# Chunked scans of a two-head block: 64x64 quadrant products against padded 128x128 products, four chains in step

## The chip, the cores and the metric

The kernel runs on one core of one Trainium2 chip. The metric is the device time of one execution in microseconds (us); a shorter time is better. The time before is the median of three runs.

## The reference, cut to what matters

One layer of a hybrid network on 384 tokens (128 context, 256 latent) of width 2048. One large projection makes all inputs; branch A is a bidirectional scan over tokens with a 64x64 state for each of 32 heads, branch B a short convolution, and both are projected out again:

```python
def step(S, inp):                      # for each direction d and head h
    r_t, w_t, k_t, v_t, a_t, b_t = inp
    sa = einsum('dbhij,dbhj->dbhi', S, a_t)
    S = S * w_t[..., None, :] + sa[..., :, None] * b_t[..., None, :] + v_t[..., :, None] * k_t[..., None, :]
    y = einsum('dbhij,dbhj->dbhi', S, r_t)
    return S, y
```

Context scans start at zero, latent scans at given states; the final context states are outputs. The reads of both directions are summed, normed by head, gated and projected.

## The kernel before, in words

**The dense stream.** Every product with a big weight is a step of one stream: a 128x128 tile of the weight against 384 tokens, as three matmuls (lines 81 to 83: high part by high, by low, low by high). A pair of column tiles has 32 steps, in four quarters of 8 steps. The weights of a quarter are loaded by SyncE, cast to the high part by ScalarE (line 88, `whi`) and subtracted to the low part by VectorE (line 89, `wlo`), with three buffers of each: a cast waits until TensorE is through with the quarter three before.

**The scans.** Heads go in 16 blocks of two. In a block each direction's 384 tokens are six chunks of 64: two of the context and four of the latent tokens. So a block has four chains: context and latent (`ch` 0 and 1), forward and backward (`d` 0 and 1). Work inside the chunks comes first: `prep_a` (rates, decays, keys; the last product is `pn`, from which VectorE makes `kn` with three reciprocals), `prep_b` (masked 64x64 matrices `A` by the products `pA`; inverses of their 32x32 corners on VectorE, by way of DRAM), `prep_c` (transposes `pv`, `pb`; products `pav`; states transposed in, `psi`). Then `scan`: the products `pH` and `pX` complete the 64x64 inverses, with copies `x11` between them; `pbn` gives the bonus `bon`. For each chunk of a chain: `po` (state by keys and reads, 128x128), an add on VectorE, `pq` (the solve), copies to `sav` on ScalarE, `pu` (the state update), and two multiply-adds for each chain on VectorE into the state `st`. Next, `py2` adds the reads inside the chunks, `pso` transposes the final context states out, and `norm` and `finish` end the block.

**Quadrants.** `pA` has 64 rows of contraction; `pq`, `pu`, `pav` and `py2` have one product for each head, whose outputs lie in 64 partitions each; `pH` and `pX` are 32x32 products. All of these are float32, and each float32 product stands as two instructions (passes) in the trace; a transpose is one.

**Order.** TensorE's order is written out by hand: `drive` runs the generators of the scans, and each `yield n` puts n dense steps (3n matmuls) into the stream before the next small burst. `PB0, PB1, H0, H1, CH0, CH1` are these numbers. The four chains are advanced two at a time: two chains' bursts, `CH0` steps, the other two chains' bursts. Between `prep_c` and `scan` lie at least `WINDOW` = 80 steps, under which the inverses run. The other engines' order is made by a scheduler when the program is built, and each engine works its list in order.

The matmuls with the dense weights in the shown code are `mm3`; `bank` is one of five PSUM banks.

Of the kernel before, what the change touches and what calls it, by code (L numbers as in the profile page):

```python
# [56 lines left out]
def hybrid_step(ctx, tc, cst, x_prompt, x_sample, state_f, state_b, c, c_ctx, ada_w, ada_b, norm_g,  # L57
# [507 lines left out]
    st = {}
    for d in range(2):
        for ch in range(2):
            s0 = sp.tile([P, P], F32, tag=f"st{d}{ch}", name=f"st{d}{ch}")
            G.memset(s0[:], 0.0)
            st[d, ch] = s0  # L570
# [83 lines left out]
    def prep_b(b, o):  # L654
        """the decayed operands and the masked matrices inside the chunks"""
        r, kk = r_[b], o["kk"]
        o["pr"], o["bk"], o["A"] = [], [], []
# [16 lines left out]
        uo = dp.tile([2, 2, 2, 12, 32, 32], F32, tag="uo", name=f"uo_{b}", bufs=2)  # L674
        for d in range(2):
            pr, bk = o["pr"][d], o["bk"][d]
            A = sp.tile([P, NCH, 2, P], F32, tag=f"A{d}", name=f"A_{b}_{d}")
            m0 = C_MB if d else C_MF
            mk = cs[:, m0:m0 + P].unsqueeze(1).broadcast_to([P, 3, P])
            for n3 in (0, 3):  # L680
                pas = [bank(f"pA_{b}_{d}_{n3}_{h}") for h in range(2)]
                for n in range(3):
                    for h in range(2):
                        TE.matmul(pas[h][:, n, :], bk[hss[h], n3 + n, :], pr[hss[h], n3 + n, :],  # L684
                                  start=True, stop=True)
# [24 lines left out]
        o["x11"] = []  # L710
        for d in range(2):
            A = o["A"][d]
            for e in range(2):
# [4 lines left out]
            nc.sync.dma_start(x11[0:32], uo[1, d, 0].rearrange("i s t -> s i t"))
            o["x11"].append(x11)

    def prep_c(b, o):
        """keys and values by token, the values' part of the removals, the bonus"""
        r, v = r_[b], v_[b]
        o["bkt"], o["sav"] = [], []
        for d in range(2):
            for h in range(2):
                nc.sync.dma_start(s_in[d][hss[h], hss[h]], ctx_st[d][0, 0, 2 * b + h])
        for d in range(2):
            sav = sp.tile([P, NCH, P], F32, tag=f"sav{d}", name=f"sav_{b}_{d}")
# [8 lines left out]
            for e in range(2):  # L738
                S.copy(sav[C:P, e:NCH:2, :], pv[C * e:C * e + C, 0:3, :])
# [1 line left out]
            o["sav"].append(sav)
        for d in range(2):
            bt = sp.tile([P, NCH, P], F32, tag=f"bt{d}", name=f"bt_{b}_{d}")
            # the last latent chunk changes no state that is read
            for n0, n1 in (((0, 3), (3, 5)), ((0, 3), (4, 6)))[d]:
# [3 lines left out]
                S.copy(bt[:, n0:n1, :], pb[:, 0:n1 - n0, :])  # L749
                yield 1  # L750
            o["bkt"].append(bt)
        for d in range(2):
            sav = o["sav"][d]
            for n3 in (0, 3):
                pv = bank(f"pav_{b}_{d}_{n3}")
                for n in range(3):
                    for h in range(2):
                        TE.matmul(pv[hss[h], n, 0:C], o["A"][d][C:P, n3 + n, h, 0:C], sav[C:P, n3 + n, hss[h]],
                                  start=True, stop=True)
                for h in range(2):  # L760
                    S.copy(sav[0:C, n3:n3 + 3, hss[h]], pv[hss[h], 0:3, 0:C])
                yield 1
# [4 lines left out]
        yield 1  # L767
        for d in range(2):
            pt = bank(f"psi_{b}_{d}")
            TE.transpose(pt[:, 0, :], s_in[d][:], ident)  # L770
            V.tensor_copy(st[d, 1][:], pt[:, 0, :])
            yield 1

    def scan(b, o):
        # upper right blocks of the 64x64 inverses, U11*A12*U22; the first product transposed
        for d in range(2):
            A, x11 = o["A"][d], o["x11"][d]
            py = bank(f"pH_{b}_{d}")
            for n in range(NCH):
                for h in range(2):  # L780
                    g = 32 * (2 * (n % 2) + h)
                    TE.matmul(py[g:g + 32, n // 2, 0:32], A[0:32, n, h, 32:64], x11[0:32, 2 * n + h, :],
                              start=True, stop=True)
# [10 lines left out]
        for d in range(2):  # L794
            A, x11 = o["A"][d], o["x11"][d]
            pz = bank(f"pX_{b}_{d}")
            for n in range(NCH):
                for h in range(2):
                    g = 32 * (2 * (n % 2) + h)
                    TE.matmul(pz[g:g + 32, n // 2, 0:32], x11[32:64, 2 * n + h, :], A[32:64, n, h, 32:64],  # L800
                              start=True, stop=True)
            for j in range(4):
                (V.tensor_copy, S.copy)[d](A[0:32, j // 2::2, j % 2, 32:64], pz[32 * j:32 * j + 32, 0:3, 0:32])
            yield H1
# [5 lines left out]
        def chain(d, ch):  # L810
            A, sav, pr, bt, ep = o["A"][d], o["sav"][d], o["pr"][d], o["bkt"][d], o["ep"][d]
            s_ = st[d, ch]
            n0 = ((0, 2), (4, 0))[d][ch]
            cnt = (2, 4)[ch]
            for i in range(cnt):
                n = n0 + i
                zero = ch == 0 and i == 0
                m = n if d == 0 else 5 - n
# [322 lines left out]
```

## Time and profile before

| | us |
|---|---|
| median of three runs (2334.58 to 2335.70) | 2335.09 |
| span of the profiled execution | 2333.0 |
| TensorE busy in the span | 2295.7 (98%) |
| VectorE busy | 1568.7 (67%) |
| ScalarE busy | 1120.9 (48%) |
| 16 blocks, from 190 to 1900 us; one block | 109.4 |

The profile is of one execution; its span leaves out what a run's time has around it (here 2.1 us against the median). PE is TensorE, DVE VectorE, ACT ScalarE, POOL GpSimd, SP SyncE. A row of the timeline has start, duration, engine, line, operation, output<-inputs, shapes and, for instructions in a row that are alike, their count and common duration. A matmul's duration is a latency: the next one starts before it ends, so what a matmul costs is read from one start to the next.

### The profile page before, as it was taken

To read this page: it belongs to the slowest core of one execution; us is meant where nothing else is said; L and a number is where in the kernel's file an instruction comes from. 1 tells how busy PE (TensorE), PEld (TensorE's weight loads), DVE (VectorE), ACT (ScalarE), POOL (GpSimd) and SP (SyncE) were. 2 spreads that over 40 slices of the span, in tenths; PEclk is the share of its full clock that TensorE was granted. 3 is DMA by queue.
4 is the path that set the end of the run, shared out by engine and by line. 5 is a ranking of instruction groups with operands and counts; after the bars stand their busy time and mean duration, and the time that the engine had idled before them with its cause. 6 is when DMAs were issued, how large, how long until landed. Compare 5 with 4: busy or idle time off the path is not lost.

```text
span 2333.0 us, 42495 instructions
## 1 busy us (share of the span) xinstructions
PE 2295.7 (98%) x16788; PEld 2043.7 (88%) x16788; DVE 1568.7 (67%) x3350; ACT 1120.9 (48%) x2342; POOL 81.6 (3%) x83
## 2 busy tenths in 40 slices
PE   5999999999999999999999999999999999999998
PEld 2579999989898989899998989898989989868988
DVE  2258777787777878787877777776868665333444
ACT  3246445454555555464645464555555543223333
POOL 2000000000000000000000000000000000000000
PEclk9999999999999999999999999999999999999999
DMA  9963433434353434343433444343444457774633
GB/s 335 344 177 106 128 103 107 134 101 126 103 138 94 124 106 127 99 121 104 130 105 107 141 116 137 109 140 100 131 118 130 144 175 243 239 257 154 226 133 119
DMA packets 431718, 340.08 MB, mean 146 GB/s; under 512 B 84816, under 2 KB 413088, under 8 KB 430624
## 3 DMA queue, kind: packets, MB, share of 16 engines
q1 hardware_dynamic: 430032, 335.62, 48.2%
q8 instruction: 132, 2.16, 0.4%
q10 hardware_dynamic: 432, 1.57, 0.2%
q14 instruction: 66, 0.54, 0.1%
q0 software_dynamic: 1056, 0.19, 0.1%
HBM read 307.37 MB, written 29.36 MB: 144 GB/s over the span
## 4 chain that ended last, share of the span: by engine, by line
PE 95%; DVE 1%; DMA 1%; SPq 1%; issue 1%; ACT 0%; POOLq 0%; POOL 0%; ACTq 0%
PE d_rk L81 4%; PE d_rk L83 4%; PE d_rk L82 4%; PE d_gv L81 3%; PE d_gv L82 3%; PE d_gv L83 3%; PE d_ma L81 3%; PE d_bc L81 3%; PE d_mb L81 2%; PE d_bg L81 2%; PE d_bx L81 2%; PE d_gb L81 2%; PE pA L684 2%; PE d_oa L81 2%; PE pada L276 2%; PE d_oa L83 2%
## 5 line engine op out<-in xcount | busy, mean ns | idle before, releaser
L701 DVE TENSOR_TENSOR ut<-U 48x30 f32<-48x30 f32 (+14 forms) x480 | 154.3, 322 | 60.6 <-DMA U<-ui 49.5
L81 PE MATMUL d_gv<-h_hi,whi_gv 128*128 128x384 f32 x496 | 165.9, 335 | 0.0
L83 PE MATMUL d_gv<-h_hi,wlo_gv 128*128 128x384 f32 x496 | 165.7, 334 | 0.0
L82 PE MATMUL d_gv<-h_lo,whi_gv 128*128 128x384 f32 x496 | 165.7, 334 | 0.0
L81 PE MATMUL d_rk<-h_hi,whi_rk 128*128 128x384 f32 x480 | 160.6, 335 | 0.6 <-ACT lst L542 0.6
L82 PE MATMUL d_rk<-h_lo,whi_rk 128*128 128x384 f32 x480 | 160.3, 334 | 0.0
L83 PE MATMUL d_rk<-h_hi,wlo_rk 128*128 128x384 f32 x480 | 160.3, 334 | 0.0
L703 DVE TENSOR_TENSOR U<-U,ut 48x30 f32<-48x30 f32 (+14 forms) x480 | 153.8, 320 | 8.9
L88 ACT CAST whi_gv<-raw_gv 128x1024 fp32r<-128x1024 f32 (+1 forms) x64 | 65.7, 1027 | 138.0 <-PE d_rk L82 96.6
L88 ACT CAST whi_rk<-raw_rk 128x1024 fp32r<-128x1024 f32 x60 | 62.9, 1050 | 112.1 <-PE d_rk L82 35.2
L838 ACT ACTIVATE ls<-st,ep 64x64 f32<-64x64 f32 x256 | 88.5, 346 | 52.3 <-DVE st L855 30.5
L89 DVE TENSOR_TENSOR wlo_rk<-raw_rk,whi_rk 128x1024 fp32r<-128x1024 f32 x60 | 73.2, 1220 | 46.3 <-ACT whi_rk L88 46.1
L89 DVE TENSOR_TENSOR wlo_oa<-raw_oa,whi_oa 128x1024 fp32r<-128x1024 f32 x32 | 39.2, 1224 | 91.0 <-ACT whi_oa L88 91.0
L81 PE MATMUL d_bc<-h_hi,whi_bc 128*128 128x384 f32 x256 | 96.9, 379 | 0.0
L81 PE MATMUL d_ma<-h_hi,whi_ma 128*128 128x384 f32 x256 | 96.8, 378 | 0.0
L81 PE MATMUL d_mb<-h_hi,whi_mb 128*128 128x384 f32 x256 | 96.6, 377 | 0.0
L81 PE MATMUL d_gb<-h_hi,whi_gb 128*128 128x384 f32 x256 | 96.1, 375 | 0.0
L81 PE MATMUL d_bx<-h_hi,whi_bx 128*128 128x384 f32 x256 | 95.2, 372 | 0.0
L844 ACT COPY sav<-pq 64x64 f32<-64x64 f32 x384 | 79.4, 207 | 32.9 <-PE pq L842 25.1
L81 PE MATMUL d_bg<-h_hi,whi_bg 128*128 128x384 f32 x256 | 95.0, 371 | 0.0
L81 PEld LDWEIGHTS d_gv<-h_hi,whi_gv 128*128 128x128 f32 x496 | 93.1, 188 | 0.2
L82 PEld LDWEIGHTS d_gv<-h_lo,whi_gv 128*128 128x128 f32 x496 | 93.1, 188 | 0.0
(317 smaller groups left out, 6726.4 us busy)
## 6 DMA issues: line engine op xcount, KB each, us to landing
raw_adah<-in_ada_w_dram SPq DMA_DIRECT2D x64, 512.0 KB, 8.0
raw_gv<-in_w_in_dram SPq DMA_DIRECT2D x62, 512.0 KB, 4.4
raw_rk<-in_w_in_dram SPq DMA_DIRECT2D x60, 512.0 KB, 5.3
raw_bc<-in_w_in_dram SPq DMA_DIRECT2D x16, 1024.0 KB, 5.4
raw_bx<-in_w_in_dram SPq DMA_DIRECT2D x16, 1024.0 KB, 5.5
raw_bg<-in_w_in_dram SPq DMA_DIRECT2D x16, 1024.0 KB, 5.5
raw_gb<-in_w_in_dram SPq DMA_DIRECT2D x16, 1024.0 KB, 5.4
raw_ma<-in_w_in_dram SPq DMA_DIRECT2D x16, 1024.0 KB, 5.4
```

Source lines behind the costliest of these rows:

```text
L81: TE.matmul(out, wh, xh, start=start, stop=False)
L82: TE.matmul(out, wh, xl, start=False, stop=False)
L83: TE.matmul(out, wl, xh, start=False, stop=stop)
L88: S.copy(hi[0:rows], src)
L89: V.tensor_tensor(lo[0:rows], src, hi[0:rows].bitcast(F32), ALU.subtract)
L276: TE.matmul(ps[g:g + 32, 0:512], cw[:, k, :], raw[:, k % 4, :], start=k < 4, stop=k >= KC - 4)
L684: TE.matmul(pas[h][:, n, :], bk[hss[h], n3 + n, :], pr[hss[h], n3 + n, :], start=True, stop=True)
L701: V.tensor_tensor(tv, U[:, 0:s, s:s + 1].broadcast_to([48, s, w]), U[:, s:s + 1, s + 1:].broadcast_to([48, s, w]), ALU.mult)
L703: V.tensor_tensor(U[:, 0:s, s + 1:], U[:, 0:s, s + 1:], tv, ALU.add)
L838: S.mul(ls[hss[h], :], s_[hss[h], hss[h]], lam[hss[h]])
L844: S.copy(sav[0:C, n, hss[h]], pq[hss[h], 0, 0:C])
```

## The change

- The matrices of both heads and both directions stand in one tile `A[P, 12, 2, P]`, heads side by side. The lower half of its solve part is set to zero by GpSimd after `pav` (`G.memset`).
- `pq` and `pu` become one 128x128 product for each chunk (both heads; the off-diagonal 64x64 results aren't read): two passes in place of four.
- The four chains go in step: at each `i` all live chains' `po`, then `CH0` steps, all `pq`, `CH0` steps, all `pu`, `CH1` steps. For i = 0 the context chains have no `po`; for i = 2 and 3 only the latent chains live.
- `pA` goes in two bursts a block instead of four, `pav` in one instead of four, `pH` and `pX` in one each instead of two, `py2` in one instead of three, `psi` in one instead of two. `pso` moves from the end to the place ahead of `po` of i = 2.
- VectorE's adds and ScalarE's copies to `sav` take two chains at once. Half of the `x11` copies go from ScalarE to VectorE, where the ones after `pX` are again half and half.
- The DMAs that carry the 32x32 corners go by head: 8 out and 8 back a block instead of 4 and 4, and 2 for `x11`.
- `PB1, H0, H1, CH0, CH1` go from 3, 2, 1, 2, 2 to 6, 3, 3, 3, 3. Comments are dropped.

```diff
-    PB0, PB1, H0, H1, CH0, CH1 = 14, 3, 2, 1, 2, 2
+    PB0, PB1, H0, H1, CH0, CH1 = 14, 6, 3, 3, 3, 3
...
+        pz = corner("pH", lambda f, h: A[0:32, f, 0, C * h + 32:C * h + C], lambda f, h: x11[0:32, 2 * f + h, :])
+        for j in range(4):
+            (S.copy, V.tensor_copy)[j % 2](x11[32:64, j::4, :], pz[j])
+        yield H0
...
+        pz = corner("pX", lambda f, h: x11[32:64, 2 * f + h, :], lambda f, h: A[32:64, f, 0, C * h + 32:C * h + C])
...
+        for i in range(4):
...
+                for d, f in enumerate(ff):
+                    TE.matmul(po[:, 2 * a + d, :], o["pr"][d][:, f % NCH, :], st[ch][:, d, :], start=True, stop=True)
+            for a, (ch, fs, ff) in enumerate(pairs):
+                if not (ch == 0 and i == 0):
+                    V.tensor_tensor(sav[0:C, fs, :], po[0:C, 2 * a:2 * a + 2, :], sav[0:C, fs, :], ALU.add)
...
+            yield CH0
+            for a, (ch, fs, ff) in enumerate(pairs):
+                for d, f in enumerate(ff):
+                    TE.matmul(pq[:, 2 * a + d, :], A[:, f, 0, :], sav[:, f, :], start=True, stop=True)
+            for a, (ch, fs, ff) in enumerate(pairs):
+                for h in range(2):
+                    S.copy(sav[0:C, fs, hss[h]], pq[hss[h], 2 * a:2 * a + 2, hss[h]])
+            yield CH0
+            if i < 3:
...
+                        TE.matmul(pu[:, 2 * a + d, :], bt[:, f, :], sav[:, f, :], start=True, stop=True)
...
+                                V.scalar_tensor_tensor(st[ch][hs, d, hs], pu[hs, 2 * a + d, hs], lam[hs],
+                                                       lss[f][hs, :], ALU.mult, ALU.add)
+                yield CH1
+            if i == 1:
+                pt = bank(f"pso_{b}")
+                for d in range(2):
+                    TE.transpose(pt[:, d, :], st[0][:, d, :], ident)
```

How VectorE's list changes is seen at two places of block 8, and the names are the same in all middle blocks. The first is between `pn` (of the next block's `prep_a`) and the copies after `pX`. Before:

```order
L631 TENSOR_SCALAR kn_12191<-pn_12188 128x384
L646 TENSOR_SCALAR kd_0_12201<-sig_2_12168,par,omka 128x384
L633 RECIPROCAL kn_12191<-kn_12191 128x128 x3
L792 TENSOR_TENSOR bon_12262<-pbn_12259,v_10837 128x384
L803 COPY A_0_11523<-pX_0_12264 32x3x32 x4
```

And now, where `x_8` is the tile `x11`:

```order
L630 TENSOR_SCALAR kn_11512<-pn_11509 128x384
L645 TENSOR_SCALAR kd_0_11522<-sig_2_11489,par,omka 128x384
L632 RECIPROCAL kn_11512<-kn_11512 128x128
L791 COPY x_8_10994<-pH_11534 32x6x32
L632 RECIPROCAL kn_11512<-kn_11512 128x128
L798 TENSOR_TENSOR bon_11575<-pbn_11572,v_10242 128x384
L791 COPY x_8_10994<-pH_11534 32x6x32
```

The second `x11` copy, without which `pX` can't go past its third product, stands behind two reciprocals and behind `bon`, which needs `pbn`.

The second place is from the add after the latent chains' first `po` to the first state updates. Before:

```order
L827 TENSOR_TENSOR rhs_0_2_12317<-po_0_2_12315,sav_0_11685 64x128
L827 TENSOR_TENSOR rhs_1_0_12325<-po_1_0_12323,sav_1_11706 64x128
L647 TENSOR_TENSOR kd_0_12201<-k_11958,kd_0_12201 128x384
L648 TENSOR_TENSOR sig_2_12168<-kn_12191,sig_2_12168 128x384
L641 SCALAR_TENSOR_TENSOR L_1_12205<-cs,sig_1_12144 128x384
L89 TENSOR_TENSOR wlo_bc_0_0_12284<-raw_bc_0_12281,whi_bc_0_0_12283 128x1024
L646 TENSOR_SCALAR kd_1_12209<-sig_3_12180,par,omka 128x384
L662 TENSOR_TENSOR bk_0_12690<-sig_2_12168,sig_0_12132 128x6x64
L853 TENSOR_SCALAR st_1113<-pu_0_0_12369,ep_1125 64x64 x2
L853 TENSOR_SCALAR st_1117<-pu_1_4_12374,ep_1127 64x64 x2
```

And now:

```order
L827 TENSOR_TENSOR sav_11009<-po_0_11626,sav_11009 64x2x128
L647 TENSOR_TENSOR sig_2_11489<-kn_11512,sig_2_11489 128x384
L89 TENSOR_TENSOR wlo_bc_0_0_11612<-raw_bc_0_11609,whi_bc_0_0_11611 128x1024
L645 TENSOR_SCALAR kd_1_11530<-sig_3_11501,par,omka 128x384
L661 TENSOR_TENSOR bk_0_11924<-sig_2_11489,sig_0_11453 128x6x64
L646 TENSOR_TENSOR kd_1_11530<-k_11279,kd_1_11530 128x384
L647 TENSOR_TENSOR sig_3_11501<-kn_11512,sig_3_11501 128x384
L662 TENSOR_TENSOR bk_0_11924<-kd_0_11522,sig_0_11453 128x6x64
L661 TENSOR_TENSOR bk_1_11930<-sig_3_11501,sig_1_11465 128x6x64
L662 TENSOR_TENSOR bk_1_11930<-kd_1_11530,sig_1_11465 128x6x64
L871 SCALAR_TENSOR_TENSOR st_1115<-pu_0_11665,ep_1121,ls_2_11631 64x64 x2
L871 SCALAR_TENSOR_TENSOR st_1115<-pu_0_11665,ep_1123,ls_6_11634 64x64 x2
```

Nine operations that have nothing to do with the scan stand between the add and the state updates, where six stood. Of the eight state updates of a step only the first waits for TensorE, and it waits for the whole burst `pu`.

More of the change, by code (lines that the diff above doesn't have):

```diff
@@ L562, in hybrid_step @@
     ps1 = ctx_sc.enter_context(tc.tile_pool(name="ps1", bufs=1, space=bass.MemoryType.PSUM))
[L565 to L570, printed above, removed]
+    st = []
+    for ch in range(2):
+        s0 = sp.tile([P, 2, P], F32, tag=f"st{ch}", name=f"st{ch}")
+        G.memset(s0[:], 0.0)
+        st.append(s0)
     s_in = []
@@ L738, in prep_c @@
             for e in range(2):
[L739 removed]
+                S.copy(sav[C:P, NCH * d + e:NCH * d + NCH:2, :], pv[C * e:C * e + C, 0:3, :])
             yield 1
[L741 removed]
         for d in range(2):
[L743 to L745 removed]
+            for n0, n1 in (((0, 4), (4, 5)), ((0, 3), (4, 6)))[d]:
                 pb = bank(f"pb_{b}_{d}_{n0}")
@@ L748, in prep_c @@
                     TE.transpose(pb[:, n - n0, :], o["bk"][d][:, n, :], ident)
-                S.copy(bt[:, n0:n1, :], pb[:, 0:n1 - n0, :])
+                S.copy(bt[:, NCH * d + n0:NCH * d + n1, :], pb[:, 0:n1 - n0, :])
                 yield 1
-            o["bkt"].append(bt)
-        for d in range(2):
[L753 to L762, printed above, removed]
+        pvs = [bank(f"pav_{b}_{d}") for d in range(2)]
+        for f in range(2 * NCH):
+            for h in range(2):
+                TE.matmul(flat(pvs[f // NCH][hss[h]])[:, C * (f % NCH):C * (f % NCH) + C], A[C:P, f, 0, hss[h]],
+                          sav[C:P, f, hss[h]], start=True, stop=True)
+        for d in range(2):
+            for h in range(2):
+                S.copy(sav[0:C, NCH * d:NCH * d + NCH, hss[h]],
+                       flat(pvs[d][hss[h]])[:, 0:NCH * C].rearrange("p (n i) -> p n i", i=C))
+        G.memset(A[C:P, :, 0, :], 0.0)
+        yield 2
         ks = o["kd"]
@@ L793, in scan @@
         o["bon"] = bon
[L794 to L804, printed above, removed]
+        pz = corner("pX", lambda f, h: x11[32:64, 2 * f + h, :], lambda f, h: A[32:64, f, 0, C * h + 32:C * h + C])
+        for j in range(4):
+            (S.copy, V.tensor_copy)[j % 2](A[0:32, j // 2::2, 0, C * (j % 2) + 32:C * (j % 2) + C], pz[j])
+        yield H1
         ytok = sp.tile([P, 3, P], F32, tag="ytok", name=f"ytok_{b}")
@@ L808, in scan @@
         written = set()
[L810 to L818, printed above, removed]
-                q, e = m // 2, m % 2
-                rhs = sav[0:C, n, :]
-                lam = ep[:, n, C:C + 1]
-                need_state = ch == 0 or i < cnt - 1
-                if not zero:
-                    po = ps1.tile([P, 512], F32, tag="A", name=f"po_{b}_{d}_{n}", bufs=5)
-                    TE.matmul(po[:, 0:P], pr[:, n, :], s_[:], start=True, stop=True)
-                    rhs_t = sp.tile([C, P], F32, tag="rhs", name=f"rhs_{b}_{d}_{n}", bufs=2)
-                    V.tensor_tensor(rhs_t[:], po[0:C, 0:P], rhs, ALU.add)
-                    rhs = rhs_t
-                    dst = ytok[C * e:C * e + C, q, :]
+        for i in range(4):
+            pairs = []
+            for ch in (1, 0):
+                if i < (2, 4)[ch]:
+                    n0 = [((0, 2), (4, 0))[d][ch] + i for d in range(2)]
+                    f0, step = n0[0], NCH + n0[1] - n0[0]
+                    pairs.append((ch, slice(f0, f0 + step + 1, step), [f0, f0 + step]))
+            po = bank(f"po_{b}_{i}")
+            pq = bank(f"pq_{b}_{i}")
+            for a, (ch, fs, ff) in enumerate(pairs):
+                if ch == 0 and i == 0:
+                    continue
+                for d, f in enumerate(ff):
[3 more added lines that the diff above has]
+                    V.tensor_tensor(sav[0:C, fs, :], po[0:C, 2 * a:2 * a + 2, :], sav[0:C, fs, :], ALU.add)
+            lss = {}
+            for a, (ch, fs, ff) in enumerate(pairs):
+                for d, f in enumerate(ff):
+                    if ch == 0 and i == 0:
+                        continue
+                    if (ch, i) != (1, 3):
+                        ls = sp.tile([P, C], F32, tag="lam", name=f"ls_{b}_{f}", bufs=4)
+                        lam = o["ep"][d][:, f % NCH, C:C + 1]
+                        for h in range(2):
+                            S.mul(ls[hss[h], :], st[ch][hss[h], d, hss[h]], lam[hss[h]])
+                        lss[f] = ls
+            for a, (ch, fs, ff) in enumerate(pairs):
+                for d, f in enumerate(ff):
+                    if ch == 0 and i == 0:
+                        continue
+                    m = f if d == 0 else 5 - f % NCH
+                    dst = ytok[hss[m % 2], m // 2, :]
@@ L859, in scan @@
-        live = [chain(0, 1), chain(1, 1), chain(0, 0), chain(1, 0)]
-        while live:
-            k = 0
-            for ch in list(live):
-                if next(ch, 1):
-                    live.remove(ch)
-                    if len(live) == 2:
-                        yield CH1 - CH0 + 1
-                else:
-                    k += 1
-                if k == 2 or (k and ch is live[-1]):
-                    yield CH0 if len(live) > 2 else CH1
-                    k = 0
+            yield CH0
@@ new lines, in scan @@
+            if i == 1:
+                pt = bank(f"pso_{b}")
+                for d in range(2):
+                    TE.transpose(pt[:, d, :], st[0][:, d, :], ident)
+                for d in range(2):
+                    nst = sp.tile([P, C], F32, tag="ns", name=f"ns_{b}_{d}")
+                    for h in range(2):
+                        S.copy(nst[hss[h], :], pt[hss[h], d, hss[h]])
+                    nc.sync.dma_start(ctx_ns[d][0, 0, 2 * b:2 * b + 2].rearrange("h i j -> (h i) j"), nst[:])
@@ L877, in scan @@
                     for e in range(2):
-                        n = 2 * q + e if d == 0 else 5 - 2 * q - e
-                        TE.matmul(py[hss[e], q, hss[h]], o["A"][d][:, n, h, C:P], o["sav"][d][:, n, hss[h]],
+                        f = 2 * q + e if d == 0 else NCH + 5 - 2 * q - e
+                        TE.matmul(py[hss[e], q, hss[h]], A[:, f, 1, hss[h]], sav[:, f, hss[h]],
                                   start=d == 0, stop=d == 1)
-            yield 1
+        yield 1
         V.tensor_tensor(ytok[:], ytok[:], py[:, 0:3, :], ALU.add)
-        for d in range(2):
-            pt = bank(f"pso_{b}_{d}")
-            TE.transpose(pt[:, 0, :], st[d, 0][:], ident)
-            nst = sp.tile([P, C], F32, tag="ns", name=f"ns_{b}_{d}")
-            for h in range(2):
-                S.copy(nst[hss[h], :], pt[hss[h], 0, hss[h]])
-            nc.sync.dma_start(ctx_ns[d][0, 0, 2 * b:2 * b + 2].rearrange("h i j -> (h i) j"), nst[:])
     def norm(b, o):
```

113 lines of the change are left out of this document (53 added, 60 removed).

## Prediction

> **What bounds the kernel now.** I read the page's busy times first, then the engines' busy time by stretch, then TensorE's waits, then the timeline of one block. Page, stretch (the 16 blocks; the second row is block 7's scan from its first `po` to `py2`), and the longest waits of TensorE inside the blocks:
>
> ```profile
> span 2333.0 us, 42495 instructions
> ## 1 busy us (share of the span) xinstructions
> PE 2295.7 (98%) x16788; PEld 2043.7 (88%) x16788; DVE 1568.7 (67%) x3350; ACT 1120.9 (48%) x2342; POOL 81.6 (3%) x83
> ```
>
> ```profile
> 190.00:1900.00 1710.00, 1708.10 (x13457) 1575.20 (x13457) 1304.23 (x2919) 905.97 (x1989) 58.69 (x31) 1.00 0.43 120
> ```
>
> ```profile
> 1030.35:1056.37 26.02, 26.02 (x209) 22.28 (x208) 22.21 (x55) 17.05 (x53) 0.00 (x0) 1.00 0.29 86
> ```
>
> ```profile
> PE pA L684 <- DVE bk L662: 1.0, 1, 1.0
> PE pq L842 <- DVE rhs L827: 0.3, 1, 0.3
> ```
>
> TensorE is busy for 1708.1 of the blocks' 1710 us at full clock: every passage of a small burst costs its whole time, and nothing else sets the end. But in the scan VectorE (the third busy time of a stretch's row) is busy too, 22.2 of 26.0 us. A product that has to wait for VectorE there costs as much as one that is too long.
>
> **What a burst costs.** A dense matmul first: these are the first and the last of 58 rows 0.173 us apart (57 intervals in 9.88 us).
>
> ```profile
> 999.68 0.33 PE L83 MATMUL d_gv<-h_hi,wlo_gv 128*128 128x384 f32 x1
> ...
> 1009.56 0.33 PE L83 MATMUL d_gv<-h_hi,wlo_gv 128*128 128x384 f32 x1
> ```
>
> A burst costs the time from the dense matmul ahead of it to the second one behind it, less two dense matmuls (0.35). Five bursts follow: `pq` and `po` of two chains, `py`, `pA`, `pH`, each with those two neighbours.
>
> ```profile
> 1033.29 0.34 PE L83 MATMUL d_bc<-h_hi,wlo_bc 128*128 128x384 f32 x1
> 1033.56 0.45 PE L842 MATMUL pq<-rhs,A 64*64 64x64 f32 x8
> ...
> 1034.22 0.34 PE L82 MATMUL d_bc<-h_lo,whi_bc 128*128 128x384 f32 x1
> ```
>
> ```profile
> 1030.17 0.34 PE L83 MATMUL d_bc<-h_hi,wlo_bc 128*128 128x384 f32 x1
> 1030.35 0.61 PE L825 MATMUL po<-st,pr 128*128 128x128 f32 x4
> ...
> 1030.97 0.34 PE L82 MATMUL d_bc<-h_lo,whi_bc 128*128 128x384 f32 x1
> ```
>
> ```profile
> 1056.10 0.34 PE L83 MATMUL d_bx<-h_hi,wlo_bx 128*128 128x384 f32 x1
> 1056.37 0.69 PE L879 MATMUL py<-sav,A 128*64 128x64 f32 x16
> ...
> 1057.26 0.34 PE L82 MATMUL d_bx<-h_lo,whi_bx 128*128 128x384 f32 x1
> ```
>
> ```profile
> 1070.60 0.34 PE L83 MATMUL d_bg<-h_hi,wlo_bg 128*128 128x384 f32 x1
> 1070.87 0.94 PE L684 MATMUL pA<-pr,bk 64*128 64x128 f32 x12
> ...
> 1072.01 0.34 PE L82 MATMUL d_bg<-h_lo,whi_bg 128*128 128x384 f32 x1
> ```
>
> ```profile
> 1026.17 0.34 PE L83 MATMUL d_bc<-h_hi,wlo_bc 128*128 128x384 f32 x1
> 1026.44 0.39 PE L782 MATMUL pH<-x,A 32*32 32x32 f32 x24
> ...
> 1027.04 0.34 PE L82 MATMUL d_bc<-h_lo,whi_bc 128*128 128x384 f32 x1
> ```
>
> So `pq` (8 passes) costs 0.93 - 0.35 = 0.58, `py` (16) 1.16 - 0.35 = 0.81, `pA` (12) 1.06, `pH` (24) 0.52, `po` (4) 0.45. Between `pq` and `py` eight passes add 0.23, 0.029 each; the rest of `pq`, 0.58 - 8 x 0.029 = 0.35, is what entering and leaving a burst of part-array products costs. With that fixed part a pass of `pA` costs 0.06 and one of `pH` 0.007. `po`, full-array, costs 4 x 0.1135 and has no fixed part to speak of.
>
> **The gain on TensorE, a block.** All of it lies on the path.
> - `pq`: 6 bursts of 0.58 = 3.50; now 12 products, 24 passes of 0.1135 = 2.72. Gain 0.78.
> - `pu`: 10 chain steps. By my reading of the code its form and passes are those of `pq`, so 5 x 0.58 = 2.92; now 20 passes, 2.27. Gain 0.65.
> - `pav`, 4 bursts of 12 passes like `pq`'s: 4 x 0.70 = 2.80; now one of 48: 0.35 + 48 x 0.029 = 1.74. Gain 1.06.
> - `py2`: 3 x 0.81 = 2.44; now one of 48, 1.74. Gain 0.70.
> - `pA`: 4 x 1.06 = 4.25; now 2 of 24: 2 x (0.35 + 1.44) = 3.58. Gain 0.7.
> - `pH` and `pX`: 4 x 0.52 = 2.10; now 2 of 48: 2 x (0.35 + 0.34) = 1.38. Gain 0.7.
> - `po`, `pso`, `psi`: the same passes, nothing.
>
> Together 4.6 us a block, 16 x 4.6 = 74 us. Bounds: 68 to 78, if a pass in a burst of 48 costs 10% more or the fixed part is 0.37.
>
> The Trainium skill, page "TensorEngine Tiling (Array Packing)", section "Performance Considerations", advises to tile the array wherever contraction and columns are 64 or less, since tiles work at the same time; by it the padding of `pq` and `pu` is a step the wrong way. What the rows make of it: per chain step four tiled passes add 0.115 and two full ones 0.227, so padding alone loses 0.11; it wins only because each tiled burst pays 0.35 at its ends. If full products paid that too, 7 bursts x 0.35 x 16 = 39 us of the 74 would go.
>
> **What now comes late.** With pairs of chains out of step, one pair's copies and updates lay under the other pair's burst and four dense steps. With all in step there are only three dense steps, 9 x 0.173 = 1.56 us, between a burst and the one that needs its result, and twice as many results. The durations for three places:
>
> ```profile
> 1024.43 0.34 PE L628 MATMUL pn<-sqh,bones_r 128*128 128x384 f32 x1
> 1024.87 0.39 PE L782 MATMUL pH<-x,A 32*32 32x32 f32 x24
> 1024.98 0.56 DVE L631 TENSOR_SCALAR kn<-pn 128x384 f32<-128x384 f32 x1 [0.53 <-PE pn L629]
> 1025.45 0.47 DVE L646 TENSOR_SCALAR kd<-sig,par,omka 128x384 f32<-128x384 f32 x1
> 1025.84 2.57 DVE L633 RECIPROCAL kn<-kn 128x128 f32<-128x128 f32 x3
> ...
> 1028.46 0.56 DVE L792 TENSOR_TENSOR bon<-pbn,v 128x384 f32<-128x384 f32 x1
> ...
> 1028.93 1.07 DVE L803 COPY A<-pX 32x96 f32<-32x96 f32 x4
> ```
>
> ```profile
> 1030.77 0.51 DVE L827 TENSOR_TENSOR rhs<-po,sav 64x128 f32<-64x128 f32 x2 [0.30 <-PE po L825]
> ```
>
> ```profile
> 1045.06 1.18 DVE L855 SCALAR_TENSOR_TENSOR st<-pu,ep,ls 64x64 f32<-64x64 f32 x4 [0.56 <-PE pu L849]
> ```
>
> ```profile
> 1024.17 1.28 ACT L643 ACT_TABLE_LOAD   x1
> ```
>
> ```profile
> L88 ACT CAST whi_rk<-raw_rk 128x1024 fp32r<-128x1024 f32 x60 | 62.9, 1050 | 112.1 <-PE d_rk L82 35.2
> ...
> L89 DVE TENSOR_TENSOR wlo_rk<-raw_rk,whi_rk 128x1024 fp32r<-128x1024 f32 x60 | 73.2, 1220 | 46.3 <-ACT whi_rk L88 46.1
> ```
>
> The last two are groups of the page: a cast lasts 1.05 us, a `wlo` 1.22.
>
> **Place 1, `pX`.** Count from `pn` at 0. VectorE: `kn` at 0.55, the rates at 1.02, a reciprocal at 1.41 (0.86 each), the first `x11` copy at 2.27 (0.26), a reciprocal until 3.39, `bon` 0.47 more, the second copy until 4.1. TensorE: `pH` at 0.44, 0.69 with its fixed part, nine dense 1.56: `pbn` at 2.7, `pX` due at 3.1. Wait 1.0 us (0.8 to 1.3), new, in the 14 middle blocks.
>
> **Place 2, the second `po`.** Count from the first `po` (4 passes, 0.45). With 1.56 after each burst, `pq` (8 passes, 0.91) starts at 2.0, `pu` at 4.5, the next `po` at 6.95, and its fourth product, at 7.6, needs the last state update. VectorE: the add is through by 1.1 (`po` ends at 0.61; two single adds take 0.51); then eight operations 0.47 apart, as `bon` and the row after it, and a `wlo`: 3.8 + 1.2, free at about 6.0. `pu` ended at 5.5, so the updates start at 6.0. Eight of them 0.30 apart end at 8.4, and the product starts at 8.5. Wait 0.9 (0.4 if VectorE were free, 1.1 if it starts 0.2 late), in the 14 middle blocks.
>
> **Place 3, `pso`.** It now stands ahead of the third `po` and needs all eight updates. From the second `pq` at 0: `pu` at 2.47, ended by 3.5; updates until 5.9 at the earliest; the second transpose is due at 2 x 2.47 + 0.11 = 5.05. Wait 0.9 in every block. In five middle blocks a `wlo` stands ahead of the updates whose cast has to wait until TensorE is two dense steps past `pq`: 2.1 + 1.05 + 1.22 = 4.4, updates until 6.8, wait 1.75; in two others a gate product stands there that waits for ScalarE's last copies, about 2.2. In seven blocks ScalarE loads a table (1.28) ahead of the copies that `pu` needs; I count 0.4 there, between nothing and the whole load. 5 x 1.75, 2 x 2.2, 9 x 1.0 and 7 x 0.4 make 25 us, 1.6 a block (0.9 to 2.2).
>
> Sum: 16 x (1.0 + 0.9 + 1.6) = 56, less 2 for the end blocks: 54 us (34 to 74 by the bounds). Elsewhere I find cover: copies to `sav` (four, at 0.26 as the copies after `pX`, an estimate) end at 1.06 + 1.04 after an eight-pass burst begins, 0.3 before `pu`; the inverses come back early, though ten DMAs go where six went:
>
> ```profile
> 1016.64 0.47 SPq L718 DMA_DIRECT2D x<-uo  x1
> ```
>
> That is the last of the six, issued 8.2 us before `pH` (1024.87); four more at about 0.45 take 1.8 of them. If that cover went, `pH` would wait once a block. GpSimd's memset has the whole window.
>
> **How the numbers follow.** 2333.0 - 74 + 54 = 2313 for the profiled span; the median lies 2.1 above the span, so 2315 us. Cases:
> - The forecast, a gain cut to between 5 and 40 us by late updates (2295 to 2330): 0.60.
> - Gain and waits even out within 0.2%, 4.7 us, about what a measurement of this kernel can tell from no change: 0.12.
> - Slower: place 3 decides. From 4.6 - 1.9 = 2.7 us there the waits eat the whole gain, and a further 0.3 a block shows. It would be so if VectorE, in order, waits for ScalarE's late results in all blocks as in those two: at 3.5 us, 16 x 5.4 - 2 = 84, 10 more than the gain, 2345. For it: VectorE is 85% busy in the scan. Against it: in four middle blocks only 1.5 us of other work stands there. 0.16.
> - The waits hardly appear, because the operations in between end earlier than I count: gain 40 to 74, 2261 to 2295. Against it: the 0.9 of place 3 needs nothing but the updates themselves. 0.10.
> - The tiling rule's case: full products pay the fixed part too: 2315 + 39 = 2354. Against it stands the `po` row. 0.02.
>
> Faster 0.70, same 0.12, slower 0.18. The likeliest case's own range is 2295 to 2330; the range for 8 in 10 goes from the low bounds (2333 - 78 + 34 + 2 = 2291) a little into the fourth case, and from the high ones (2333 - 68 + 74 + 2 = 2341) into the slower one: 2288 to 2346.
>
> **What would show it.** Right: bursts of `pq` and `pu` with 4 or 8 passes at 0.11 and no fixed part; one `pav` and one `py2` burst a block of about 1.7; waits of TensorE for VectorE at `pX` (`x11`), `po` and `pso`, 1 to 2 us each and some 54 in all, where there were none. Wrong: waits for ScalarE's copies, at `pH` for a DMA or in the dense stream for `wlo`; or bursts of 48 passes that cost in proportion.

## The result and the profile after

The changed kernel takes 2359.64 us (median of 4 runs, 2356.57 to 2360.24) against 2335.16 for the kernel before beside it (2334.58 to 2335.70): ratio 1.0101, 95% interval 1.0087 to 1.0116. It is 24 us slower. The forecast was 2315, with 2288 to 2346 as its range: the time lies above the range, and the sign was wrong.

The page after, its stretch of the 16 blocks, and TensorE's longest waits from the blocks on (for whom, us in total, times, longest; those for `d_ob` lie around the last block):

```profile
span 2357.1 us, 40814 instructions
PE 2264.2 (96%) x16084; PEld 2086.1 (89%) x16084; DVE 1568.0 (67%) x3254; ACT 1060.2 (45%) x1958; POOL 101.9 (4%) x97
```

```profile
190.00:1900.00 1710.00, 1656.17 (x12679) 1594.12 (x12677) 1290.14 (x2806) 843.93 (x1621) 77.02 (x46) 0.99 0.42 118
```

```profile
PE pX L785 <- DVE x L791: 19.2, 14, 1.4
PE pso L878 <- DVE st L871: 17.9, 32, 1.5
PE po L824 <- DVE st L871: 6.9, 14, 0.8
PE d_ob L83 <- DVE wlo_ob L89: 3.0, 3, 1.2
```

TensorE, busy for 1708 of these 1710 us before, now stands idle for 54, most of it for VectorE, and the granted clock reads 0.99 where it read 1.00. The list counts only full idleness. A product that is issued and held counts as busy, so costs are taken as in the prediction: from the dense matmul ahead of a burst to the second one behind it, less 0.35.

**The saving came.** `pq` of four chains and `py2`, each with those neighbours (block 7; start, us, engine, line):

```profile
1041.75 0.34 PE L83 MATMUL d_bc<-h_hi,wlo_bc 128*128 128x384 f32 x1
1041.93 1.05 PE L853 MATMUL pq<-sav,A 128*128 128x128 f32 x8
...
1043.00 0.34 PE L82 MATMUL d_bc<-h_lo,whi_bc 128*128 128x384 f32 x1
...
1069.35 0.34 PE L83 MATMUL d_bx<-h_hi,wlo_bx 128*128 128x384 f32 x1
1069.62 1.62 PE L891 MATMUL py<-sav,A 128*64 128x64 f32 x48
...
1071.45 0.34 PE L82 MATMUL d_bx<-h_lo,whi_bx 128*128 128x384 f32 x1
```

1.25 - 0.35 = 0.90 and 2.10 - 0.35 = 1.75, where 0.91 and 1.74 were forecast. Costed so, and without what stands in them as a wait, all bursts of the 16 blocks take 73 us less than before.

**The waits are larger, and one is new.** Place 1, `pX` in block 7 (timeline):

```profile
1032.97 0.34 PE L627 MATMUL pn<-sqh,bones_r 128*128 128x384 f32 x1
...
1034.38 0.94 DVE L632 RECIPROCAL kn<-kn 128x128 f32<-128x128 f32 x1
...
1035.35 0.35 DVE L791 COPY x<-pH 32x192 f32<-32x192 f32 x1
...
1035.73 0.95 DVE L632 RECIPROCAL kn<-kn 128x128 f32<-128x128 f32 x1
...
1036.10 0.26 PE L785 MATMUL pX<-A,x 32*32 32x32 f32 x6
1036.72 0.56 DVE L798 TENSOR_TENSOR bon<-pbn,v 128x384 f32<-128x384 f32 x1
1037.31 0.36 DVE L791 COPY x<-pH 32x192 f32<-32x192 f32 x1
...
1037.72 0.57 PE L785 MATMUL pX<-A,x 32*32 32x32 f32 x42 [1.37 <-DVE x L791]
```

`pX` starts 3.13 after `pn`, as forecast (3.1), and stops after a few products until 4.75. Place 2, the second `po`:

```profile
1044.39 1.05 PE L862 MATMUL pu<-sav,bt 128*128 128x128 f32 x8
...
1045.88 0.54 DVE L662 TENSOR_TENSOR bk<-kd,sig 128x384 f32<-128x384 f32 x1
1046.34 1.22 DVE L871 SCALAR_TENSOR_TENSOR st<-pu,ep,ls 64x64 f32<-64x64 f32 x4
...
1047.08 2.29 PE L824 MATMUL po<-st,pr 128*128 128x128 f32 x8
1047.60 1.23 DVE L869 TENSOR_SCALAR st<-pu,ep 64x64 f32<-64x64 f32 x4
```

Eight passes, 0.90 of work, last 2.29: `po` is held for the fourth state. The new one is the fourth `po` of a block:

```profile
1061.69 0.26 ACT L856 COPY sav<-pq 64x128 f32<-64x128 f32 x1
1061.98 1.05 ACT L88 CAST whi_bx<-raw_bx 128x1024 fp32r<-128x1024 f32 x1
1062.06 0.66 PE L862 MATMUL pu<-sav,bt 128*128 128x128 f32 x4
...
1063.06 1.23 DVE L89 TENSOR_TENSOR wlo_bx<-raw_bx,whi_bx 128x1024 fp32r<-128x1024 f32 x1 [3.36 <-ACT whi_bx L88]
...
1064.32 1.23 DVE L871 SCALAR_TENSOR_TENSOR st<-pu,ep,ls 64x64 f32<-64x64 f32 x4
1065.06 1.03 PE L824 MATMUL po<-st,pr 128*128 128x128 f32 x4 [0.77 <-DVE st L871]
```

VectorE is idle for 3.36 us, longer than `pu` takes to come: a `wlo` stands ahead of the updates in its queue, and the cast of that `wlo` stands on ScalarE behind the copies from `pq`.

Summed over the blocks, cost less unwaited cost: `pX` 23 us (14 of 1.6), the second `po` 19, `pso` with the third `po` 24, the fourth `po` 15. Together 81, where the prediction had 54.

**The clock drops behind the gaps.** Block 6 (timeline, then the stretch behind):

```profile
926.96 0.57 PE L785 MATMUL pX<-A,x 32*32 32x32 f32 x42 [1.37 <-DVE x L791]
...
928.11 0.52 PE L83 MATMUL d_bx<-h_hi,wlo_bx 128*128 128x384 f32 x1
928.43 0.52 PE L81 MATMUL d_bx<-h_hi,whi_bx 128*128 128x384 f32 x1
...
930.35 0.95 PE L824 MATMUL po<-st,pr 128*128 128x128 f32 x4
```

```profile
927.60:931.00 3.40, 3.40 (x13) 3.40 (x14) 2.74 (x6) 2.60 (x5) 0.00 (x0) 0.51 0.00 0
```

Dense matmuls are 0.32 apart here instead of 0.173. The trace of after has seven such stretches of 3.41 us before its last matmuls, that of before none. Five follow a wait at `pX` (the others one at `pso` and one at `d_ob`) and cover the first `po` of their block, which costs 0.84 to 1.15 there and 0.45 in every other block. VectorE gains time on TensorE in those five: the second `po` behind them waits 0.6 to 0.8 us instead of 1.5.

### The profile page after: what moved, and what is told of

Its sections match the earlier page's. It is cut to its first block, busy times and chain, and to the rows that moved or that the text cites. A ratio compares the mean times of both kernels' runs of the same rounds, so it can differ in the third digit from the quotient of the medians.

```text
span 2357.1 us, 40814 instructions
## 1 busy us (share of the span) xinstructions
PE 2264.2 (96%) x16084; PEld 2086.1 (89%) x16084; DVE 1568.0 (67%) x3254; ACT 1060.2 (45%) x1958; POOL 101.9 (4%) x97
## 4 chain that ended last, share of the span: by engine, by line
PE 80%; DVE 13%; DMA 2%; issue 2%; ACT 1%; SPq 1%; POOLq 0%; POOL 0%; DVEq 0%; ACTq 0%
PE d_rk L81 4%; PE d_rk L83 4%; PE d_rk L82 4%; PE d_gv L81 3%; PE d_gv L82 3%; PE d_gv L83 3%; DVE st L871 3%; PE d_oa L81 2%; PE pA L683 2%; PE pada L276 2%; PE d_oa L83 2%; PE d_oa L82 2%; PE d_bx L81 2%; PE d_ma L81 2%; PE d_bx L83 2%
## 5 line engine op out<-in xcount | busy, mean ns | idle before, releaser
L83 PEld LDWEIGHTS d_gv<-h_hi,wlo_gv 128*128 128x128 f32 x496 | 93.1, 188 | 0.2 <-DVE wlo_gv L89 0.2
L81 PE MATMUL d_bc<-h_hi,whi_bc 128*128 128x384 f32 x256 | 91.9, 359 | 0.0
L81 PEld LDWEIGHTS d_rk<-h_hi,whi_rk 128*128 128x128 f32 x480 | 90.1, 188 | 0.9 <-ACT lst L542 0.9
```

Of the source, the lines that this page charges most:

```text
L81: TE.matmul(out, wh, xh, start=start, stop=False)
L83: TE.matmul(out, wl, xh, start=False, stop=stop)
```

## The experiments

Theory A: the saving is there, and late VectorE results eat it. Theory B: the saving is not there. The fourteen kernels (e9 leaves out the low parts of the weights):

| kernel | us, median (lowest to highest) |
|---|---|
| before, beside these runs | 2334.0 to 2335.6 |
| changed | 2359.64 (2356.57 to 2360.24) |
| e1, four dense steps | 2357.26 (2352.44 to 2363.5) |
| e2, `pH`'s copies on ScalarE | 2332.27 (2330.47 to 2335.0) |
| e3, `pso` at the end | 2333.56 (2329.75 to 2335.38) |
| e6, e2 and e3 together | 2305.87 (2304.67 to 2306.25) |
| e4, pairs out of step | 2324.41 (2321.4 to 2326.86) |
| e5, e4 and e2 together | 2297.73 (2293.52 to 2300.57) |
| e7, e5 with tiled `pq`, `pu` | 2299.14 (2296.59 to 2303.36) |
| e8, e6, every second cast on GpSimd | 2353.07 (2350.06 to 2356.16) |
| e9, e6 without low parts | 2280.83 (2278.58 to 2282.45) |
| e10, e6, steps 2/3/4 | 2305.75 (2304.36 to 2310.41) |
| e11, e5, steps laid by hand | 2318.34 (2315.82 to 2319.11) |
| e12, e11 tiled | 2309.21 (2307.73 to 2311.15) |
| e13, e6, `bk` on GpSimd | 2337.69 (2336.32 to 2340.91) |
| e14, e5, `bk` on GpSimd | 2317.22 (2312.26 to 2319.39) |

**e1: more cover.**

```diff
-    PB0, PB1, H0, H1, CH0, CH1 = 14, 6, 3, 3, 3, 3
-    PRO, WINDOW, FIRST, LAST = 32, 80, 28, 16
+    PB0, PB1, H0, H1, CH0, CH1 = 14, 6, 3, 3, 4, 4
+    PRO, WINDOW, FIRST, LAST = 32, 69, 28, 16
```

> The changed kernel with four dense steps instead of three after each of po, pq and pu (0.52 us more each; the window ahead of the scan gives back the 11 steps). Theory A, late results: TensorE waits for VectorE's updates; a cycle of po, pq and pu is 1.56 us longer, so the waits at the second po (about 1.3), at pso (1.5) and at the fourth po (1.0) shrink to 0.3 or less each, pX keeps its 1.6: 14 x 1.3 + 16 x 1.2 + 14 x 1.0 = 51 us less, 2300 to 2320. Theory B, the merged bursts and the full-array products do not save the 74 us that I counted: the order of dense steps changes nothing, 2350 to 2365.

Measured 2357, 37 above theory A's range. Its waits:

```profile
PE pH L785 <- DMA x<-uo: 31.3, 19, 5.3
PE pso L878 <- DVE st L871: 5.6, 18, 1.2
PE pX L785 <- DVE x L791: 4.7, 7, 1.4
```

The waits for updates did shrink (`pso` from 17.9, `po` gone from the list). The 5.7 us a block that the window gave up were the cover of the inverses' DMAs, and `pH` now waits for those: the same steps cannot cover both. The clock reads 0.989, the lowest of the profiled executions. The time lies in B's range, so the run alone does not decide against B; the next two do, and so do the burst costs above.

**e2: place 1 alone.**

```diff
-            (S.copy, V.tensor_copy)[j % 2](x11[32:64, j::4, :], pz[j])
+            S.copy(x11[32:64, j::4, :], pz[j])
...
+        pz = corner("pX", lambda f, h: x11[32:64, 2 * f + h, :], lambda f, h: A[32:64, f, 0, C * h + 32:C * h + C])
...
         bon = sp.tile([P, T], F32, tag="bon", name=f"bon_{b}")
         V.tensor_tensor(bon[:], pbn, v_[b][:], ALU.mult)
```

(`pX` and its copies, which stood behind `bon`, move ahead of it)

> The changed kernel with all four copies of pH's result on ScalarE and the bonus product (bon) behind the copies of pX. Theory A: the wait at pX, 1.6 us in 14 blocks, is for VectorE's two copies, which stand behind reciprocals and bon; it falls to 0.3 or less: 2337 to 2345. Rival: pX waits for the inverses' DMAs or for ScalarE's copies anyway: no change, 2355 to 2362.

2332: 27 us less, and 5 below theory A's range, which had left out the clock. The waits of `pX`, 23 us, are gone, and of the seven stretches of half clock one is left. Part of that gain is given back: with `pX` early, `pso` waits more (20.6 instead of 17.9).

**e3: place 3 alone.**

```diff
-            if i == 1:
-                pt = bank(f"pso_{b}")
...
         V.tensor_tensor(ytok[:], ytok[:], py[:, 0:3, :], ALU.add)
+        pt = bank(f"pso_{b}")
...
```

> The changed kernel with the transposes of the final states (pso) back behind the block's last burst, where they stood before. Theory A as predicted at place 3: pso needs all eight updates, the third po behind it only the first four, which end 1.2 us earlier: 16 x 1.2 = 19 us less, about 2341. Rival: the same wait comes back at the third po, because what holds VectorE up stands ahead of all eight updates: 2352 to 2360. Theory B: no change, 2355 to 2362.

2334: 26 us less, rather more than the 19. Of the 24 us at place 3 some 5 stay with the third `po`, 19 go; and the fourth `po` waits 0.7 in most blocks instead of 1.0, another 5. ScalarE has the copies of `pso` no longer ahead of its next cast: in block 7 the cast starts 1.94 us after `pq` in the changed kernel and 1.20 after it in e6, where `pso` also stands at the end.

**e6: both, chains in step.** The two diffs together.

> The changed kernel, chains in step, with both single edits: pH's copies on ScalarE with bon late, and pso at the end. Theory A: the two waits are separate, 2359.6 - 27 - 26 = 2306, 2300 to 2312, and the waits at the second po (1.4 in 15 blocks) and the fourth (1.0 in 14) stay. Rival: the waits feed each other, and one comes back at the next burst: 2318 to 2332.

2306, as expected to the microsecond: the two waits are separate. What is left here is 1.35 at the second `po`, about 0.5 at the third, 0.7 at the fourth.

**e4 and e5: the pairs of chains out of step.** The scan's loop becomes a generator for a pair, and two of them take turns:

```diff
+        live = [pair(1), pair(0)]
+        while live:
+            for p in list(live):
+                if next(p, 1):
+                    live.remove(p)
+                else:
+                    yield CH0 if len(live) > 1 else CH1
```

with CH0 = CH1 = 2 and WINDOW = 81.

> The changed kernel with all its merged bursts and full-array products, but the two pairs of chains out of step again, a burst of each in turn with two dense steps between (and pso at the end, as before). Full-array products have no fixed part, so splitting their bursts costs nothing. Theory A: the 74 us stay, the waits at po and pso (about 60 us) go, the wait at pX stays (23): 2333 - 74 + 23 + 2 = 2284, 2275 to 2300. Theory B: the saving on TensorE is not there: 2330 or more.

> Pairs of chains out of step and pso at the end, and now all copies of pH's result on ScalarE with bon behind the copies of pX. Theory A: the wait at pX (1.6 us in 14 blocks, 24 in all) goes, and with it the nine stretches of half clock of 3.41 us that followed it (about 1.7 lost in each, 15): 2324 - 24 - 15 = 2285, 2275 to 2295. Rival: what the wait at pX hides comes out at the first po behind it, which waits 0.7 already in nine blocks: 2300 to 2312.

e4 gave 2324, 40 above its number, e5 2298, 13 above. In e4 the expectation had counted no waits at `po` and no half clock: there are 25 us of the first (0.3 at nearly every `po` of the pair that runs last alone, 0.6 to 1.3 at one or two more a block) and nine stretches of the second. In e5 the stretches are gone from the blocks, the waits at `po` are not (26 us); the list names

```profile
PE po L822 <- DVE st L856: 5.6, 11, 0.9
```

Out of step is better than in step by 8 us (e5 against e6): 29 us of waits are left against 38.

**e7: are the full products worth it?** e5 with, for `pu` likewise:

```diff
-                    TE.matmul(pq[:, d, :], A[:, f, 0, :], sav[:, f, :], start=True, stop=True)
+                    for h in range(2):
+                        TE.matmul(pq[hss[h], d, hss[h]], A[0:C, f, 0, hss[h]], sav[0:C, f, hss[h]],
+                                  start=True, stop=True)
```

> The kernel with pairs out of step and pH's copies on ScalarE, but pq and pu again as 64-column products of one head each on a part of the array. By my count a burst of eight such passes costs 0.58 where four full passes cost 0.45: 11 bursts x 16 blocks x 0.13 = 23 us more than the same kernel with full products. Rival (padding wastes the array): no slower, or up to 20 us faster.

No slower: 2299 against 2298. Yet the bursts cost what I had counted: 176 tiled bursts take 0.58 each, the full ones 0.45, 23 us in all. The waits at `po` are 20 us smaller with tiled products, and 3 more go at `pX`. While a longer burst runs, VectorE comes nearer to its end. Where VectorE sets the end, the 23 us saved on `pq` and `pu` are worth nothing.

**e8: the late cast.**

```diff
-        S.copy(hi[0:rows], src)
+        (nc.gpsimd.tensor_copy if th == 'whi' and nm.endswith('_1') and 'sp' in box else S.copy)(hi[0:rows], src)
```

> Chains in step with both single edits, and every second cast of a dense weight (whi) on GpSimd instead of ScalarE from the scans on. Theory A: at the fourth po VectorE is late because a wlo stands ahead of the updates whose cast stands on ScalarE behind the copies from pq; with the cast on GpSimd the 1.0 us in 14 blocks go, 14 us less than the kernel with both edits. Rival: GpSimd needs longer for the cast than ScalarE with its queue, or the updates themselves set the wait: no gain, or 10 to 60 us slower.

2353, 47 slower; the rival's case. A cast on GpSimd takes 1.2 to 2.2 times as long as on ScalarE, by group (two groups of this kernel: busy, mean ns):

```profile
L88 POOL CAST whi_rk<-raw_rk 128x1024 fp32r<-128x1024 f32 x29 | 46.4, 1600 | 127.0 <-PE d_rk L82 88.2 <-PE d_bx L82 12.3 <-DVE U L706 7.1
L88 ACT CAST whi_rk<-raw_rk 128x1024 fp32r<-128x1024 f32 x31 | 32.5, 1052 | 12.3 <-issue 7.5 <-PE d_ma L82 2.9 <-PE d_mb L82 1.5
```

and the second `po` waits 3.1 to 3.6 in the middle blocks. It says nothing about the cast at the fourth `po`.

**e9: no `wlo` at all.** It tells that apart. From the scans on `lo` is the tile of `hi`:

```diff
+                S.copy(hi[:], raw[:, 4 * q:4 * q + 4, :])
+                res.append((hi, hi))
```

> Chains in step with both single edits, and the low parts of the dense weights left out from the scans on: whi stands in their place, so TensorE does the same work and VectorE loses some 230 wlo of 1.2 us. Theory A1, VectorE is late at the second, third and fourth po because of the wlo that stand among its scan work: the waits left there (15 x 1.35 + 16 x 0.45 + 14 x 0.68 = 37 us) go: 2266 to 2275. Theory A2, what is late is the updates themselves, eight of them 0.30 apart against three dense steps: the second po keeps about 0.9, and 22 us go: 2280 to 2290. Theory B, VectorE is not what TensorE waits for: no change, 2304 to 2308.

2281, the number of A2, in a way that needs both: the waits at the fourth `po` and at the third (but for two blocks) are gone to the last 0.01, so those were the `wlo`; the second `po` still waits 1.27. Block 5 of this kernel there:

```profile
797.88 1.10 PE L869 MATMUL pu<-sav,bt 128*128 128x128 f32 x8
...
798.77 0.55 DVE L669 TENSOR_TENSOR bk<-kd,sig 128x384 f32<-128x384 f32 x1
...
799.24 0.54 DVE L773 TENSOR_TENSOR kd<-kd,kd 128x384 f32<-128x384 f32 x1
799.71 1.22 DVE L878 SCALAR_TENSOR_TENSOR st<-pu,ep,ls 64x64 f32<-64x64 f32 x4
```

The updates start 1.83 after `pu`, behind the next block's preparation.

**e10, e11, e12: the same steps, laid elsewhere.** e10 is e6 with two dense steps after `po`, three after `pq`, four after `pu`; e11 is e5 with

```diff
+        live, steps = [pair(1), pair(0)], [2, 1, 2, 2, 2, 3, 2, 2, 2, 2, 4, 1, 2, 3, 1, 2]
```

and e12 is e11 with the tiled products of e7.

> Chains in step with both single edits, and the same nine dense steps of a cycle laid otherwise: two after po, three after pq, four after pu (three each before). Theory A2: after pu eight updates of 0.30 have 1.56 us of cover, after po one or two additions of 0.42 have as much; a step moved is 0.52 off each wait behind pu: 15 x 0.52 + 9 x 0.5 + 14 x 0.5 = 19 us less than the 2306 of the kernel with both edits, 2282 to 2292. Theory A1, VectorE's queue is late as a whole: the wait only moves to pq, 2300 to 2308.

> Pairs out of step with pH's copies on ScalarE, and the dense steps laid by hand where the waits are: three ahead of the po that waits 0.5, four behind the last pu in which both pairs run (its po waits 0.3 to 1.5), one after po and three after pu in the last pair's cycle (waits 0.3). One step more in all, taken from the window. Theory A2: 14 x 0.5 + 14 x 0.9 + 16 x 0.3 = 24 us of waits, of which 20 go: 2298 - 20 = 2278, 2272 to 2288. Theory A1: they move to pq, 2294 to 2300.

> The kernel with the dense steps laid by hand, but pq and pu as 64-column products on parts of the array. If padding saved 0.13 a burst but lost the saving to waits (tiled and full kernels took 2299 and 2298 without the laying), it now shows: 2278 + 23, less what waits are left in the full one, 2294 to 2302. Rival: the padding is worth nothing on TensorE: as the full one, within 4 us.

e10 changed nothing, e11 lost 21 us against e5. TensorE waits at another product, first e10, then e11:

```profile
PE pq L853 <- DVE sav L827: 10.7, 25, 0.9
```

```profile
PE pq L841 <- DVE sav L823: 27.4, 31, 1.9
```

The addition between `po` and `pq` is short (0.42), but it queues on VectorE behind a `wlo`, which may itself wait for its cast. In e11 a `wlo` stands directly ahead of the addition at the 14 longest of these waits (1.4 to 2.7 us by cost), and in 12 of them it had waited for its cast. So the wait moved, as A1 had said, and a step taken away after `po` comes back at `pq`; but e11 lies above the ranges of A1 and A2 both. e12, expected at 2294 to 2302, is above that too, and 9 us faster than its full twin, where I had counted the tiled bursts 23 slower: the longer bursts are cover again.

**e13 and e14: what stands ahead of the updates.**

```diff
-            V.tensor_tensor(bk[:, :, 0:C], c3(bn[:]), c3(em[:]), ALU.mult)
-            V.tensor_tensor(bk[:, :, C:P], c3(kd[:]), c3(em[:]), ALU.mult)
+            G.tensor_tensor(bk[:, :, 0:C], c3(bn[:]), c3(em[:]), ALU.mult)
+            G.tensor_tensor(bk[:, :, C:P], c3(kd[:]), c3(em[:]), ALU.mult)
```

> Chains in step with both single edits, and the next block's four decayed keys (bk, 0.47 us each on VectorE) on GpSimd. In the trace four of them stand between the first po's additions and the updates, and the updates start 0.9 us after pu has ended. Theory A3, VectorE is late at the second po by this other work: the wait falls from 1.35 to about 0.45 in 14 blocks, 13 us less than the 2306 of the kernel with both edits, 2288 to 2298. Theory A2, the updates alone: no change, 2303 to 2309. Rival: GpSimd needs so long for bk that the decayed products (pA) wait: slower, 2310 to 2330.

> Pairs out of step with pH's copies on ScalarE, and bk on GpSimd. Theory A3: the waits left at po there (26 us in all, 0.5 at the first pair's and 0.3 to 1.4 at the last pair's) shrink by about a third, 2285 to 2293. Theory A2: no change, 2295 to 2300. Rival: pA waits for GpSimd, 2302 to 2325.

Both lose, 32 and 19 us, and not at `pA`; e13 lies above all its ranges, e14 at the rival's time but not for its reason. The same place in block 5, e6 first:

```profile
803.44 1.19 DVE L89 TENSOR_TENSOR wlo_gb<-raw_gb,whi_gb 128x1024 fp32r<-128x1024 f32 x1
...
805.45 1.05 PE L862 MATMUL pu<-sav,bt 128*128 128x128 f32 x8
...
807.29 1.22 DVE L871 SCALAR_TENSOR_TENSOR st<-pu,ep,ls 64x64 f32<-64x64 f32 x4
```

```profile
813.41 1.60 POOL L661 TENSOR_TENSOR bk<-sig,sig 128x384 f32<-128x384 f32 x1 [0.50 <-DVE sig L647]
814.13 1.97 DVE L89 TENSOR_TENSOR wlo_gb<-raw_gb,whi_gb 128x1024 fp32r<-128x1024 f32 x1
...
815.83 1.23 PE L862 MATMUL pu<-sav,bt 128*128 128x128 f32 x8
...
818.26 1.25 DVE L767 SCALAR_TENSOR_TENSOR kd<-kd,par,r 128x384 f32<-128x384 f32 x1
819.05 1.31 POOL L661 TENSOR_TENSOR bk<-sig,sig 128x384 f32<-128x384 f32 x1
819.43 1.22 DVE L871 SCALAR_TENSOR_TENSOR st<-pu,ep,ls 64x64 f32<-64x64 f32 x4
```

VectorE's operations beside a GpSimd product become longer (the `wlo` 1.97 for 1.19), and other work has moved into the place of `bk`. The updates start 3.60 after `pu` instead of 1.84, and the wait at the second `po` goes from 1.35 to 2.9. So the remedy failed, but it measured how place 2 depends on that start. In block 0, where nothing stands ahead, the updates start 1.09 after `pu` and `po` waits 0.61; at 1.84 (e6) it waits 1.35, at 1.97 (ten blocks of the changed kernel) 1.48, at 3.60 (e13) 2.9. The wait is 0.6 for the eight updates themselves and then, nearly one for one, how late they start.

## Why the prediction was wrong, point by point

- **The gain on TensorE, 74 us (68 to 78)**: right, 73. Full-array products have no fixed part (0.45 for four passes, 0.90 for eight), and merging takes the fixed 0.35 once; the case in which full products pay it too did not occur. What was wrong was the sentence beside it, "All of it lies on the path": e5 and e7 differ by 23 us of bursts and by nothing in time.
- **The step that failed is the sum of the waits**, "54 us (34 to 74 by the bounds)": 81. (Its own terms give 52: the two end blocks, without places 1 and 2, take off 3.8 and not 2.) Place 3, `pso`, was right (1.6 forecast, 1.5 measured). Three terms were not:
  - Place 1 was the right mechanism with too short operations: "Wait 1.0 us (0.8 to 1.3)", measured 1.6. Queue spacing was used (reciprocal 0.86, copy 0.26, `bon` 0.47) where single operations last 0.95, 0.35 and 0.56; five of them lie in the chain.
  - Place 2, "Wait 0.9 (0.4 if VectorE were free", is 1.48 in ten blocks. With VectorE free the eight updates cost 0.6, and they start 0.9 later than that, behind the next block's preparation.
  - The fourth `po` had no line at all. The mechanism was described, a `wlo` in front of the updates whose cast is late, but only for `pso` and for some blocks. ScalarE's queue at the last step of the scan was not looked at; the moved `pso` puts its copies into it as well. It measured 15 us, 1.0 to 1.4 in 14 blocks.
- **Cover claimed elsewhere**: the inverses' DMAs held, as claimed, and so did the copies to `sav`, but for 0.27 us at two `pu`. But the dense stream now waits for its own `wlo` and casts, 7.5 us at block 0 and around the last block, where it was 2.0.
- **The clock** was not in the sum. Seven stretches of 3.41 us at half speed cost at most 7 x 1.7 = 12 us, of which some 7 show in dense matmuls (seven of them a stretch, 0.147 too long each) and 3 at the first `po` of five blocks.
- Together: -73 + 81 + 5.5 + 10 = +23.5; the span grew by 24.1.
- **The rival on the slower side** had the right sign and the right reason in part (VectorE, in order, waiting for ScalarE), with the wrong place: not 2.7 at `pso`, but 0.6 more at each of the two other places and 1.0 at a new one. A range made from the bounds of three places holds only if the list of places is complete.

The Trainium skill, page "TensorE: Matmul & The Clock Gate", Part 1, says that the clock is gated to half by an activity window of 3413 ns that runs free of the kernel. The trace agrees in both: stretches last 3.41 us, and their starts in the changed kernel lie 27, 130, 130, 97, 32 and 52 such windows apart, to a thousandth. It differs in what it takes: by the Trainium skill the array goes cold after a whole idle window; here an idle time of 1.37 us was enough, and of fourteen gaps alike at `pX` five were followed by a stretch. Windows laid off from those starts hold eight of the fourteen gaps whole. The five are among them and start 0.2 to 1.5 us into their window; the other three start 1.8 us into theirs, and the six split between two windows had no stretch. So a whole gap in one window seems to be needed and is not enough; what decides was not tried by itself.

## What to carry to other kernels

A saving on the engine that sets the end is worth only what the next engine in the chain can follow: before merging steps of dependent chains, list for every product which result it needs, what stands ahead of that result in its engine's queue, and what that in turn waits for, to the last step of the loop. Price operations in such a chain by their own duration and not by their spacing in a queue. When a wait is covered by moving filler, look first at whose cover the filler was (e1: the DMAs'; e10 and e11: the addition's).

The fastest kernels that keep the low parts are e5 (ratio to before 0.9839, interval 0.9825 to 0.9854) and e7 (0.9848, 0.9834 to 0.9863), ahead of e6 (0.9874): merged small bursts, pairs out of step, `pH`'s copies on ScalarE and `pso` at the end. Padding `pq` and `pu` added nothing to that, and the four chains in step (e6) took 8 us more.

## What the runs showed of the hardware

- A gap of 1.4 us on TensorE can cost another 1.7 us behind it, half a stretch of 3.41 us at half speed. With the wait at `pX` gone (e2, e5, e6), one stretch of half clock is left, behind two gaps close together of 1.7 to 2.8 us in sum.
- VectorE beside GpSimd: a `wlo` of 1.19 us took 1.97 while GpSimd multiplied two tiles (e13), and the 18 of them beside such a product last 1.84 on average, the others 1.26. Beside GpSimd casts (e8) the `wlo` stays at 1.25, and the cast is the one that takes long: 2.68 us on average beside a `wlo`, 1.24 without one. The Trainium skill, page "SBUF — State Buffer", section "SBUF: two separate sides", has the two engines share a pair of ports that one instruction holds for its whole length; the longer times agree with that, though no run here tries it alone.
